# Who multiplies the modulation tiles, and where constants are made, in the opening of a decoder trunk

## The chip, the cores and the metric

One Trainium2 chip, one of its cores. The metric is the device time of one execution in microseconds (us); lower is better. TensorE is called PE here and in the profile (PEld is its weight load), VectorE DVE, ScalarE ACT, GpSimd POOL, SyncE SP.

## The reference, cut to what matters

One decoder layer over 2048 positions of 1024 channels, float32. Six modulation vectors come from the conditioning vector `c`; the first two, shift and scale, act on the input of the first projection:

```python
c_act = silu(c)                                  # 1024
mod = c_act @ ada_w + ada_b                      # ada_w: 1024 x 6144
sh1, sc1, g1, sh2, sc2, g2 = split(mod, 6)
h = rmsnorm(x, norm_mix_w) * (1.0 + sc1) + sh1   # 2048 x 1024
proj = h @ w_in                                  # split into eleven parts
# A: gated linear recurrence, B: sparse attention by an index score and top-k, C: convolution
x = x + g1 * (concat[o_a, o_b, o_c] @ w_out)
h = rmsnorm(x, norm_mlp_w) * (1.0 + sc2) + sh2
x = x + g2 * (relu(h @ mlp_w1)**2 @ mlp_w2)
out = rmsnorm(x, final_norm_w)
```

## The kernel before, in words

The 2048 positions go in four blocks of 512. Every large product is made of three rounded products: each operand is split into a high part, rounded for PE's fast float32 format by ACT, and a low part, what the rounding left. The low part of a weight tile (`wlo`, L318) is made by POOL; that of a slice of activations (`al`, L288) by DVE for slices 1, 4 and 6 and by POOL for the others.

**The opening** (block 0, before the projection runs). `in_norm` loads four tiles of x, and ACT, POOL and DVE normalise them. The scale `a1` and the shift `sh1` are columns of 128 channels by 8. `ada_half` makes half of one of them: eight tiles of `ada_w`, 128 rows by 512 columns, are multiplied by the matching column of `cact`, summed over the tiles and then over the rows. Before the change DVE multiplies and adds tile 0 and tiles 3 to 7 (`acc`, L238, L240). Tiles 1 and 2 (`AK`) are multiplied by ACT (L233) and added by POOL (L236). Then `part_sum` (L226) sums over the rows on PE: the tile is the stationary operand and a column of ones the moving one, four matmuls for 512 columns, each shown as two in the records. It runs twice in each half, once for POOL's tile and once for `acc`. DVE adds the bias (L244).

The order is: near half of the scale (`a1`, channels 0 to 511), near half of the shift (`sh`), then slices 0 to 3 of the input (`to_act_steps`: four transposes on PE, L281; scale and shift on ACT, `tf`, L286; rounding on ACT, `ah`, L287; low part). With them PE runs the first half of the channels of the first two projection units (`KO` = 2, L424). Then the far halves of scale and shift, slices 4 to 7, and the second half of these two units. `tf` has two buffers.

**The projection** of a block is a list of units, `in_units`: unit 0 the index key, 1 and 2 the index queries, 3 the forget gate of the recurrence's first head, 4 its query, 5 its values (wide), 6 its output gate, and so on. A unit fetches 512 KB of weights, ACT rounds them (L317), POOL makes their low parts, PE multiplies, ACT and DVE evacuate. `next_w` splits the weights of a unit about one unit ahead of its use. Rounded weights of block 0 are also written to DRAM (`wk_d`) for the later blocks. Behind unit 6 the recurrence of the first head starts in the background (`hgrn_gen`); it uses the masks `lmask`. The first top-k search (`topk_gen`) uses `zq` and `gq_`.

**Constants.** `late_consts`, called at unit 1, makes the constants of the search (`search_consts`: iota and two powers on POOL, some fifteen small DVE instructions), loads the convolution's taps, forms the bounds of the forget gate, and makes five masks: for each level DVE fills `mwork`, POOL selects twice (L514, L516), DVE casts into `lmask` (L518).

**Order.** The program is a list of instructions with tiles; a scheduler orders each engine's queue by a modelled timeline, taking the earliest instruction of the program that is ready, and tiles of one tag share a fixed number of buffers. So an instruction can stand well before its place in the program, and each queue then runs strictly in that order. DMAs are issued from SP, apart from a few small ones on ACT's queue.

Of the kernel before, what the change touches and what calls it, by code (L numbers as in the profile page):

```python
# [16 lines left out]
OP = mybir.AluOpType  # L17
# [26 lines left out]
KO, NPF = 2, 2  # L44
AK = [1, 2]
PTB, PM, LB, LB2 = 1, 1, 4, 4
# [32 lines left out]
def trunk(ctx, tc, x, c, ada_w, ada_b, norm_mix_w, norm_mlp_w, w_in, hg_lb_logits,  # L79
# [136 lines left out]
    def ada_half(sec, c0, dst, key, slots):  # L216
# [4 lines left out]

        side = []

        def part_sum(t, vec, first, last):
# [4 lines left out]
        for k in range(NK):  # L229
            t = slots[k]()  # L230
            dma(t, ada2[k * P:(k + 1) * P, sec * D + c0:sec * D + c0 + TB])
            if k in AK:
                A.mul(t, t, cact[:, k:k + 1])  # L233
                side.append(t)
                if len(side) > 1:
                    G.tensor_tensor(side[0], side[0], t, OP.add)  # L236
            elif k == 0:
                V.tensor_scalar(acc, t, cact[:, 0:1], None, op0=OP.mult)  # L238
            else:
                V.scalar_tensor_tensor(acc, t, cact[:, k:k + 1], acc, op0=OP.mult, op1=OP.add)  # L240
        if side:
            part_sum(side[0], ones[:, 0:1], True, False)
        part_sum(acc, ones[:, 0:1], not side, True)
        V.tensor_tensor(dst[:, t0:t0 + n], pt[:, :n], col("adab", sec * 8 + t0, n), OP.add)  # L244
# [29 lines left out]

    def to_act_steps(xh, acol, bcol, ah, al, mid=None):
        for k in range(NK):
# [10 lines left out]
            A.copy(hi, tf)  # L287
            (V if k in (1, 4, 6) else G).tensor_tensor(lo, tf, hi.bitcast(F32), OP.subtract)  # L288
            guard.__exit__(None, None, None)
# [176 lines left out]
    def search_consts():  # L466


        w = hp.tile([P, 5, 14], F32, tag="cu", bufs=2, name="sconst")
        ii = hp.tile([P, 14], mybir.dt.int32, tag="fb", bufs=FBB, name="sint")  # L470
        na, p_, q_, a_, b_ = [w[:, i] for i in range(5)]
# [21 lines left out]
    def late_consts():  # L493
        search_consts()
        cvrow = hp.tile([TAPS, 256], F32, tag="hc0", bufs=1, name="cvrow")
# [12 lines left out]

        mwork = hp.tile([P, 256], F32, tag="r", bufs=1, name="mwork")
        for l in range(5):  # L510
# [590 lines left out]
    def first_units(xts):  # L1101
        act = [], []
        steps = to_act_steps(xts, a1, sh1, *act)
        ws = []
# [14 lines left out]
    def in_block(b, xts, nxt):  # L1119
        act = first_units(xts) if b == 0 else to_act(xts, a1, sh1, lambda: pump("fast", rates["fast"]))  # L1120
        for u, (pieces, ev, m) in enumerate(in_units):
# [6 lines left out]
            if u == 1 and b == 0:  # L1128
                late_consts()
            if b == 0 and u < len(early):  # L1130
                ps = early[u]
# [537 lines left out]
```

## Time and profile before

| | us |
|---|---|
| median of 3 runs | 2896.21 |
| lowest, highest | 2892.06, 2897.85 |
| profiled execution, its time | 2887.88 |
| its span in the profile | 2886.1 |
| PE busy | 2757.0 (96%) |
| PEld busy | 2297.4 (80%) |
| DVE busy | 1671.6 (58%) |
| ACT busy | 1240.7 (43%) |
| POOL busy | 1086.6 (38%) |

The profiled execution is 8.3 us below the median of the runs. Busy time is an average over the whole span; the opening, where the change lies, is the first 70 us of it. Of the 40 slices of 72 us into which the page cuts the span, PE is busy five tenths in the first and nine or more in nearly all others.

### The profile page before, as it was taken

Reading aid. Unit: us, or ns where it says so; the run is one execution under the profiler, and the core shown is the slowest. Engines: PE = TensorE matmul, PEld = TensorE weight load, DVE = VectorE, ACT = ScalarE, POOL = GpSimd, SP = SyncE. Lnnn points to the kernel's source line nnn. Section 1 sums busy time; section 2 is a strip of 40 time slices with the busy share of each in tenths; the row PEclk is TensorE's granted clock in tenths of the full one; section 3 lists DMA queues with packets and bytes.
Section 4 is the critical chain, followed back from the end, with each engine's and each line's share of the span. In section 5 each row is a group of like instructions: output and inputs, shape, how many; then the busy total and the mean of one; then the engine's idle time right before and its main releaser. Section 6 shows DMA issues by size and latency. Waiting matters only on the chain.

```text
span 2886.1 us, 42799 instructions
## 1 busy us (share of the span) xinstructions
PE 2757.0 (96%) x14116; PEld 2297.4 (80%) x14116; DVE 1671.6 (58%) x3514; ACT 1240.7 (43%) x2630; POOL 1086.6 (38%) x1051
## 2 busy tenths in 40 slices
PE   5999998999999989999999999999999999999997
PEld 4888887888788777888777888888788887777876
DVE  6695697777465437657757637477662221254455
ACT  4436444533311354555556444354643333343333
POOL 7434111212100445666665222234422223345444
PEclk9999999999999989999999999999999999999999
DMA  8987676777555667889888776677867666686676
GB/s 292 293 270 248 216 233 195 221 222 248 190 187 179 224 223 252 282 287 288 291 271 290 237 223 213 208 248 257 285 219 234 204 225 204 219 283 210 229 238 207
DMA packets 428075, 688.62 MB, mean 239 GB/s; under 512 B 43384, under 2 KB 171453, under 8 KB 427837
## 3 DMA queue, kind: packets, MB, share of 16 engines
q1 hardware_dynamic: 427680, 685.67, 73.0%
q8 instruction: 113, 1.85, 0.3%
q14 instruction: 126, 1.02, 0.1%
q10 hardware_dynamic: 156, 0.07, 0.0%
HBM read 532.74 MB, written 152.84 MB: 238 GB/s over the span
## 4 chain that ended last, share of the span: by engine, by line
PE 45%; DMA 4%; DVE 4%; POOL 2%; issue 1%; ACT 1%; SPq 0%; POOLq 0%; DVEq 0%; ACTq 0%
PE mm L1306 11%; PE mm L424 10%; PE ax L424 7%; PE ax L1306 6%; PE mm L1466 3%; PE at L967 2%; PE po L1001 2%; PE at L989 1%; PE ix L809 1%; DMA wk<-wk_d 1%; DMA tr<-in_mlp_w_dram 1%; PE at L1306 1%; DVE s L816 1%; POOL wk L376 1%; DVE cum L919 1%
## 5 line engine op out<-in xcount | busy, mean ns | idle before, releaser
L424 PE MATMUL mm<-ah,wk 128*128 128x512 f32 x1920 | 509.4, 396 | 4.9 <-ACT tf L286 1.9
L424 PEld LDWEIGHTS mm<-ah,wk 128*128 128x128 f32 x1920 | 353.6, 188 | 77.7 <-ACT tf L286 2.1
L318 POOL TENSOR_TENSOR wlo<-wraw,whi 128x512 fp32r<-128x512 f32 x210 | 286.7, 1385 | 243.4 <-ACT whi L317 99.7
L999 POOL TENSOR_TENSOR pT<-L,pT 128x512 fp32r<-128x512 f32 (+3 forms) x160 | 192.9, 1207 | 371.8 <-ACT pT L998 203.1
L816 DVE SCALAR_TENSOR_TENSOR s<-r,iw_s,s 128x512 f32<-128x512 f32 (+3 forms) x266 | 237.4, 892 | 100.9 <-ACT r L811 92.8
L424 PE MATMUL mm<-al,wk 128*128 128x512 f32 x960 | 262.3, 395 | 0.0
L969 DVE CUSTOM_DVE_ANT_0 L<-at,bias 128x512 f32<-128x512 f32 (+3 forms) x152 | 93.7, 620 | 202.5 <-PE at L967 159.3
L424 PEld LDWEIGHTS mm<-al,wk 128*128 128x128 f32 x960 | 177.9, 188 | 35.4
L1306 PE MATMUL mm<-wk,hh 128*128 128x512 f32 x640 | 196.0, 395 | 2.1 <-ACT tf L286 1.1
L811 ACT ACTIVATE r<-ix 128x512 f32<-128x512 f32 (+3 forms) x256 | 133.3, 555 | 148.8 <-PE ix L809 99.9
L317 ACT CAST whi<-wraw 128x512 fp32r<-128x512 f32 x210 | 121.8, 621 | 159.7 <-DMA wraw<-in_mlp_w_dram 40.1
L273 POOL TENSOR_TENSOR hl<-hr,hh 128x512 fp32r<-128x512 f32 x96 | 128.5, 1340 | 159.9 <-ACT hh L265 158.1
L424 PE MATMUL ax<-ah,wk 128*128 128x512 f32 x720 | 185.4, 391 | 1.8 <-ACT hc L1440 1.4
L589 DVE SCALAR_TENSOR_TENSOR cx<-hc,cvc,cx 128x512 f32<-128x512 f32 x232 | 174.2, 751 | 2.0
L919 DVE TENSOR_SCALAR_CACHE_REDUCE cum<-s,ssm 128x384 bf16<-128x384 f32 (+13 forms) x112 | 165.4, 1477 | 8.2 <-POOL s L820 6.1
L997 ACT COPY L<-at 128x512 f32<-128x512 f32 (+3 forms) x160 | 82.9, 522 | 175.6 <-PE at L989 174.2
L424 PEld LDWEIGHTS ax<-ah,wk 128*128 128x128 f32 x720 | 134.1, 188 | 30.2 <-ACT hc L1440 1.8
L1466 PE MATMUL mm<-wk,hc 128*128 128x512 f32 x588 | 145.0, 392 | 6.9 <-DVE acc L1474 6.1
L983 ACT ACTIVATE L<-L,nmx 128x512 f32<-128x512 f32 (+3 forms) x160 | 103.8, 650 | 98.7 <-DVE nmx L978 98.4
L1306 PEld LDWEIGHTS mm<-wk,hh 128*128 128x128 f32 x640 | 118.0, 188 | 26.8 <-ACT tf L286 1.7
L1466 PEld LDWEIGHTS mm<-wk,hc 128*128 128x128 f32 x588 | 109.4, 188 | 34.1 <-DVE acc L1474 10.0
L1306 PE MATMUL ax<-wk,hh 128*128 128x512 f32 x384 | 122.6, 397 | 1.5 <-DMA wk<-wk_d 1.1
(364 smaller groups left out, 6077.8 us busy)
## 6 DMA issues: line engine op xcount, KB each, us to landing
wk<-wk_d SPq DMA_DIRECT2D x776, 256.0 KB
wk<-wk_d SPq DMA_DIRECT2D x196, 512.0 KB
wk_d<-whi SPq DMA_DIRECT2D x210, 256.0 KB
wk_d<-wlo SPq DMA_DIRECT2D x210, 256.0 KB
wraw<-in_mlp_w_dram SPq DMA_DIRECT2D x68, 512.0 KB
kc<-sk_d SPq DMA_DIRECT2D x112, 256.0 KB
vc<-v_d SPq DMA_DIRECT2D x112, 256.0 KB
adw<-in_ada_w_dram SPq DMA_DIRECT2D x128, 128.0 KB
```

What stands on the lines that cost most here:

```text
L273: e.tensor_tensor(lo[:, i:j], src[:, i:j], hi[:, i:j].bitcast(F32), OP.subtract)
L317: A.copy(hi, src)
L318: G.tensor_tensor(lo, src, hi.bitcast(F32), OP.subtract)
L424: T.matmul(ps, ww[k], aa[k], start=(n == 0 and k0 == 0), stop=(n == len(order) - 1 and k1 == NK))
L589: V.scalar_tensor_tensor(acc if w < TAPS - 1 else total, hc[:, w:w + TB], cvc[:, m, w:w + 1], acc, op0=OP.mult, op1=OP.add)
L811: A.activation(r[:, :w], ps[:, :w], AF.Relu, scale=32.0 ** -0.5)
L816: V.scalar_tensor_tensor(s[:, c0:c0 + w], r[:, :w], iw, s[:, c0:c0 + w], op0=OP.mult, op1=OP.add)
L919: V.tensor_scalar(dump, s, t, -AIM - i * STEP, op0=OP.is_ge, op1=OP.add, accum_out=d)
L983: A.activation(lt[:, :w], lt[:, :w], AF.Exp, bias=nmx, accum_out=sm[:, cb:cb + 1])
L999: G.tensor_tensor(pT[:, :nt, 1], lv, pT[:, :nt, 0].bitcast(F32), OP.subtract)
L1306: T.matmul(ps, aa[f][:, tok * P:(tok + 1) * P], ww[i], start=(first and n == 0), stop=(last and n == 5))
L1466: T.matmul(bank[t], aa[:, k, t * P:(t + 1) * P], ww[k], start=(i in (0, 2, 4) and n == 0), stop=(n == 5), skip_group_check=True)
```

## The change

PE multiplies tiles 1, 3, 5 and 7 of each half itself: `part_sum` runs on the tile as it was loaded, with the column of `cact` in place of the ones. ACT's multiplications and POOL's sums go; DVE keeps tiles 0, 2, 4 and 6. In block 0 DVE makes the low parts of all eight slices. `search_consts` and the masks (now `level_masks`) leave `late_consts` and are called at unit 4 of block 0; their work tiles take buffers of the tag `stg` (4 buffers, shared with the evacuations of keys and queries) in place of `cu`, `fb` and `r`.

```diff
-AK = [1, 2]
+AK = [1, 3, 5, 7]
...
             if k in AK:
-                A.mul(t, t, cact[:, k:k + 1])
-                side.append(t)
-                if len(side) > 1:
-                    G.tensor_tensor(side[0], side[0], t, OP.add)
+                part_sum(t, cact[:, k:k + 1], k == AK[0], False)
             elif k == 0:
                 V.tensor_scalar(acc, t, cact[:, 0:1], None, op0=OP.mult)
             else:
                 V.scalar_tensor_tensor(acc, t, cact[:, k:k + 1], acc, op0=OP.mult, op1=OP.add)
-        if side:
-            part_sum(side[0], ones[:, 0:1], True, False)
-        part_sum(acc, ones[:, 0:1], not side, True)
+        part_sum(acc, ones[:, 0:1], False, True)
...
-    def to_act_steps(xh, acol, bcol, ah, al, mid=None):
+    def to_act_steps(xh, acol, bcol, ah, al, mid=None, on_v=(1, 4, 6)):
...
-            (V if k in (1, 4, 6) else G).tensor_tensor(lo, tf, hi.bitcast(F32), OP.subtract)
+            (V if k in on_v else G).tensor_tensor(lo, tf, hi.bitcast(F32), OP.subtract)
...
-        w = hp.tile([P, 5, 14], F32, tag="cu", bufs=2, name="sconst")
-        ii = hp.tile([P, 14], mybir.dt.int32, tag="fb", bufs=FBB, name="sint")
+        w = hp.tile([P, 5, 14], F32, tag="stg", bufs=STG, name="sconst")
+        ii = hp.tile([P, 14], mybir.dt.int32, tag="stg", bufs=STG, name="sint")
...
     def late_consts():
-        search_consts()
...
-        mwork = hp.tile([P, 256], F32, tag="r", bufs=1, name="mwork")
+    def level_masks():
+        mwork = hp.tile([P, 256], F32, tag="stg", bufs=STG, name="mwork")
...
-        steps = to_act_steps(xts, a1, sh1, *act)
+        steps = to_act_steps(xts, a1, sh1, *act, None, range(NK))
...
             if u == 1 and b == 0:
                 late_consts()
+            if u == 4 and b == 0:
+                search_consts()
+                level_masks()
```

More of the change, by code (lines that the diff above doesn't have):

```diff
@@ L220, in ada_half @@
         t0 = c0 // P
-        side = []
         def part_sum(t, vec, first, last):
```

## The prediction

> **What bounds the kernel now.** I read the page first, then busy time by ten-microsecond stages, then the opening instruction by instruction, then the groups and waits of the stages behind it.
>
> ```profile
> span 2886.1 us, 42799 instructions
> 0.00:10.00 10.00, 0.24 (x1) 0.17 (x1) 1.97 (x15) 2.20 (x3) 6.86 (x13) 1.00 0.79 273
> 10.00:20.00 10.00, 3.15 (x13) 2.57 (x13) 7.35 (x15) 7.65 (x14) 9.04 (x11) 1.00 0.93 321
> 20.00:30.00 10.00, 6.08 (x28) 5.48 (x27) 8.54 (x17) 2.34 (x5) 6.03 (x7) 1.00 0.98 269
> 30.00:40.00 10.00, 5.53 (x21) 4.24 (x20) 8.87 (x8) 4.32 (x7) 8.73 (x7) 1.00 1.06 390
> 40.00:50.00 10.00, 9.79 (x50) 8.53 (x51) 9.05 (x17) 4.33 (x8) 6.43 (x4) 1.00 0.95 299
> 50.00:60.00 10.00, 5.78 (x29) 3.90 (x28) 7.44 (x15) 5.15 (x8) 7.68 (x5) 1.00 0.81 281
> 60.00:70.00 10.00, 9.82 (x36) 7.92 (x37) 4.44 (x7) 8.01 (x16) 6.70 (x10) 0.83 0.67 206
> 70.00:80.00 10.00, 10.00 (x48) 8.15 (x47) 5.00 (x7) 5.33 (x9) 5.89 (x7) 1.00 0.95 315
> 80.00:90.00 10.00, 10.00 (x81) 9.77 (x80) 3.00 (x7) 3.31 (x7) 3.91 (x4) 1.00 1.01 339
> ```
>
> Columns of a stage: length, busy us of PE, PEld, DVE, ACT and POOL with instruction counts, granted clock, DMA share, GB/s. From 70 us on TensorE is never idle, so what the opening saves is kept as long as weights, low parts and evacuations follow. Up to 60 us it is idle 29 of 60 us, while VectorE is at 7 to 9 tenths and the DMA engines near full. (The clock column reads 1.00 even there, yet a column sum takes 1.86 at 28 us and 0.95 at 48, next fence: the array runs at half its later speed.)
>
> The opening is a chain of three milestones: the near shift column `sh` (first halves of the sections), the far one, and the second half of the two early projection units.
>
> ```profile
> 11.49 1.32 ACT L233 ACTIVATE adw<-adw,cact 128x512 f32<-128x512 f32 x2
> 28.62 1.86 PE L226 MATMUL ax<-ones,adacc 128*128 128x1 f32 x8 [2.89 <-DVE adacc L240]
> 30.52 0.16 DVE L244 TENSOR_TENSOR sh<-ax,cols 128x4 f32<-128x4 f32 x1 [1.40 <-PE ax L226]
> 31.17 4.22 POOL L318 TENSOR_TENSOR wlo<-wraw,whi 128x512 fp32r<-128x512 f32 x3
> 32.50 5.11 DVE L240 SCALAR_TENSOR_TENSOR adacc<-adw,cact,adacc 128x512 f32<-128x512 f32 x3
> 37.53 1.75 DVE L288 TENSOR_TENSOR al<-tf,ah 128x512 fp32r<-128x512 f32 x1
> 39.38 0.78 ACT L286 ACTIVATE tf<-mm,sh,a 128x512 f32<-128x512 f32 x1 [4.91 <-DVE al L288]
> 48.31 0.95 PE L226 MATMUL ax<-ones,adw 128*128 128x1 f32 x8
> 50.19 0.16 DVE L244 TENSOR_TENSOR sh<-ax,cols 128x4 f32<-128x4 f32 x1 [0.91 <-PE ax L226]
> ```
>
> A row is start, length, engine, line, tile, count, and in brackets the idle time with what ended it. Near `sh` is done at 30.7, after a VectorE chain, a column sum on PE and a gap of 1.40. Then everything runs into VectorE and POOL: three multiply-adds take 5.11, 1.70 each, while POOL is busy; the low part on VectorE starts only at 37.53, and ACT waits 4.91 for it before it can scale slice two. Far `sh` comes at 50.19.
>
> ```profile
> 51.35 2.60 POOL L480 TENSOR_TENSOR sconst<-sconst 128x14 f32<-128x14 f32 x1
> 52.44 0.69 DVE L288 TENSOR_TENSOR al<-tf,ah 128x512 fp32r<-128x512 f32 x1 [0.78 <-ACT ah L287]
> 56.42 1.26 POOL L288 TENSOR_TENSOR al<-tf,ah 128x512 fp32r<-128x512 f32 x1
> 58.70 0.78 ACT L286 ACTIVATE tf<-mm,sh,a 128x512 f32<-128x512 f32 x1 [4.04 <-DVE gq__210 L488]
> 60.17 0.50 PE L424 MATMUL mm<-ah,whi 128*128 128x512 f32 x1 [3.75 <-ACT ah L287]
> 62.00:63.00 1.00, 1.00 (x4) 0.80 (x3) 0.57 (x1) 0.81 (x2) 0.39 (x1) 0.50 0.81 190
> ```
>
> Here the search constants are in the way. POOL spends 2.60 on each of two powers, then weight low parts, and reaches the low part of a slice at 56.42; VectorE's queue holds the constants' arithmetic, ACT waits 4.04 for it, PE waits 3.75, and the array, having been idle, comes back at a clock of 0.50.
>
> **The change part by part.** Durations come from the profiled execution: 2887.9 us beside a span of 2886.1. The median of the runs is 2896.2, so 8.3 is added at the end.
>
> ```profile
> L236 POOL TENSOR_TENSOR adw<-adw,adw 128x512 f32<-128x512 f32 x4 | 6.3, 1576 | 0.1
> L281 PE MATMUL mm<-ident,xt 128*128 128x128 f32 x32 | 7.8, 379 | 8.5 <-DVE xt L435 5.5 <-ACT tf L286 3.0
> L286 ACT ACTIVATE tf<-mm,sh,a 128x512 f32<-128x512 f32 x8 | 6.0, 774 | 12.4 <-DVE al L288 5.2 <-DVE gq__210 L488 4.0 <-DVE sh L244 3.2
> L287 ACT CAST ah<-tf 128x512 fp32r<-128x512 f32 x8 | 4.7, 618 | 0.2
> L514 POOL TENSOR_SCALAR_AFFINE_SELECT mwork<-mwork 128x256 f32<-128x256 f32 x5 | 6.4, 1278 | 4.8 <-DVE a L247 2.6 <-DVE mwork L513 2.1
> L516 POOL TENSOR_SCALAR_AFFINE_SELECT mwork<-mwork 128x256 f32<-128x256 f32 x5 | 5.8, 1165 | 0.2
> 67.63 1.98 PE L424 MATMUL mm<-ah,wlo 128*128 128x512 f32 x8
> 69.44 1.98 PE L424 MATMUL mm<-ah,whi 128*128 128x512 f32 x8
> ```
>
> Groups of the first 62 us: busy time, mean ns, idle before.
>
> *Multiplication of tiles.* Gone: 8 ACT multiplies (two took 1.32 at 11.49, so 5.3), 4 POOL adds (6.3), and 8 VectorE multiply-adds (six become four in each of four halves; up to 1.70 each). New: each half makes five column sums on PE where it made two, so 12 more in all. A sum is eight matmul records: 0.95 warm (48.31), 1.86 cold (28.62). No DMA is added, removed or moved past another, so the order of tiles on SP stays.
>
> *Near half.* Three ends. Arrival: x and the 16 near tiles are 6.3 MB; the first stages move 2.73 and 3.21 MB, so the last near tile lands at 21 to 23. With a warm array the last sums take 2 more: 25. With a cold one the queue of ten sums (18.6) and eight transposes of 0.38 (3.0) starts with the first odd tile, whose copy ACT took up at 11.49: 33. I take 26.5, nearer the warm end, and say below why: 4.0 earlier than 30.5.
>
> *Low parts on VectorE.* Five of eight move from POOL. At 52.44 VectorE needs 0.69, at 37.53 under a busy POOL 1.75. POOL still splits the weights of two units here, but has neither masks nor adds. The wait of 4.91 goes; late next is ACT, with (0.774+0.618) = 1.39 for each slice.
>
> *First half of the early units and the far half.* From 26.5+2.3 (scale, round, first matmul: 52.45 follows 50.19 in the same way) PE has 24 matmuls of 0.226 (8 of them from 67.63 to 69.44), ten sums of 0.97, and two slices' transposes at the warm rate (1.3): 5.4+9.7+1.3 = 16.4, hence far `sh` at 45.2 and not 50.2. This is a price PE didn't pay before, six sums or 5.8 of it. Ends: the far tiles' arrival (12.5 MB have moved by 40 us, the 8.4 MB of tiles, x and two units' weights are 11.5) plus two sums, 41; and, with near `sh` at 33 and half speed until 40, 53 (the 2.3 to the first matmul and the 4.7 behind it do 3.5 of the 16.4, and 12.9 are left). So 5.0 earlier in all, the first 4.0 included.
>
> *Second half.* The 3.75 wait goes with the constants. So does the slow clock behind it: a mean of 0.83 over 60 to 70 us is 1.7 lost. Late next is ACT: 1.39 for a slice against six matmuls (1.36); I leave 1.0 for that. Gain 4.5.
>
> Sum of the opening: 5.0+4.5 = 9.5 us by the time the early units end (about 67).
>
> *Constants and masks behind unit four.* They used to lie in the opening; now POOL has 6.4+5.8 of selects and 2×2.6 of powers, 17.4 in all, at about 70 to 95 us, where it makes the low parts of weights. In the new tag they wait until stores of the index queries have left its four buffers, and they stand in program order before that unit's weight splits.
>
> ```profile
> 78.36 2.80 POOL L318 TENSOR_TENSOR wlo<-wraw,whi 128x512 fp32r<-128x512 f32 x2 [4.11 <-ACT whi L317]
> 82.06 0.55 PEld L1282 LDWEIGHTS mm<-wlo,ah 128*128 128x128 f32 x4
> ```
>
> POOL finishes these two tiles at 81.16 and PE loads one at 82.06: a lead of 0.9. A power in front takes 2.6 out of that, the two selects of the first level 4.2. POOL is idle for 4.1 before 78.36, and 10 less the busy time of the stages 70 to 90 makes 10.2 in all. Queued behind on POOL are weight low parts only, and PE waits for them; on VectorE the mask's casts wait for POOL, with evacuations behind them that have a spare PSUM buffer. Ends: nothing, and 17.4-0.9 = 16.5. I take 1.5, since most of the powers fit the idle 4.1.
>
> *Transfers.* The opening's gain asks the same bytes in less time.
>
> ```profile
> ACT whi L317 <- PE mm L424: 18.8, 17, 3.1
> ACT whi L317 <- DMA wraw<-in_w_in_dram: 3.3, 2, 3.0
> ```
>
> Behind the opening the DMA share is 0.95 to 1.01. What can move up is the idle share of 40 to 80 us: 0.5+1.9+3.3+0.5 = 6.2. Of 9.5 that leaves 3.3 which PE could catch up with the stream. But the rounding of weights waited on PE 17 times (18.8) and on a transfer twice (3.3) between 62 and 182 us, so PE and not the stream set the pace. Ends 0 and 3.3; I take 0.8 on top of POOL's 1.5, since both delay the same matmuls.
>
> Net: 9.5-1.5-0.8 = 7.2. Profile 2887.9-7.2 = 2880.7; with 8.3, **2889.0**.
>
> **A warm or a cold array.** The near sums hang on this.
>
> ```profile
> 1033.62:1037.03 3.41, 3.41 (x19) 3.41 (x18) 1.23 (x4) 1.56 (x3) 1.27 (x1) 0.50 0.15 14
> 1037.03:1040.45 3.42, 3.42 (x18) 2.87 (x18) 1.62 (x4) 1.43 (x3) 1.53 (x1) 1.00 0.90 363
> 1036.04 1.48 PE L696 MATMUL ax<-q,k 128*128 128x64 f32 x8
> ```
>
> A stage of 3.41 filled without a gap by transposes and short 64-column matmuls ended with the clock going from 0.50 to 1.00. The near sums of the changed kernel fill PE just as densely (a cold one takes 1.86; an odd tile comes every 1.6 to 1.9, two of 262 KB at 321 or 269 GB/s), so I take them to warm it by about 20 us. The Trainium skill, "TensorE: Matmul & The Clock Gate", Part 1, says that about 3.4 us of sustained work releases the clock, but its Part 4 says that transposes don't count as such work. The stage above speaks against Part 4. No row shows one-column sums alone in such a stage; if they count as little as that page says of transposes, the cold rival below is what happens.
>
> The Trainium skill, "SBUF — State Buffer", section "Who interferes with whom", says that a VectorE instruction with two SBUF inputs and a POOL instruction that reads SBUF exclude each other for their whole length. The 1.75 against 0.69 agrees. By the rule alone each low part on VectorE would cost 1.75 wherever POOL splits weights; two on the path make 2.1 less gain, 2891.1.
>
> **The rivals.**
>
> *PE stays cold and becomes the opening's bound.* Near `sh` at 33, far at 53 (2.8 later), the second half still gains 4.5: net 1.7 before unit four's 1.5; the stream then costs nothing. Time about 2896. For it: PE stayed slow in every sum before 40 us. Against: the gaps between those, and the stage just shown.
>
> *The slower side: POOL at unit four.* If the selects and powers stand one behind another in front of the weight low parts, PE waits up to 16.5 where I count 1.5. It decides against the change from 8.7+5.8 = 14.5 on the path (the gain without that term, plus 0.2%); at 16.5, 2896.2-8.7+16.5 = 2904. For it: the lead of 0.9, and the fixed order. Against: the levels alternate with VectorE, which leaves POOL to the weights between them.
>
> *The constants don't move.* The scheduler had drawn them from unit one into the opening; with buffers of their new tag counted free it can do so again. Then the second half keeps its wait: 2896.2-5.0+0.8 = 2892. Against: the tag's earlier tiles belong to units before them.
>
> *More than expected.* Far `sh` by arrival (41, another 4.2) and nothing lost behind: 2896.2-13.7 = 2882.5.
>
> **How the numbers follow.** The forecast 0.44, with its own range 2886 to 2892 (nothing lost to the stream and little at unit four, or the whole 3.3 of the stream). Cold array 0.27 around 2896. POOL 0.13, from 2898 up to 2904. Constants unmoved 0.05, 2892. More 0.11, near 2882. Besides, the queues' order is worked out anew for the whole kernel, and a stall like the 3.75+1.7 can appear or go elsewhere: 5.5 either way, inside the range. Range 2882 to 2900, which leaves out about 2 in 10: part of the best case, part of POOL's. About 0.2%, 5.8 us, is what measurement can tell from no change; so faster means under 2890.4: most of the forecast (0.38) and all of the better case, with a little of the unmoved: 0.50. Slower, over 2902: most of POOL's and a little else, 0.13. Same: 0.37.
>
> **What would show it.** Near `sh` at 25 to 28 and far at 44 to 47; column sums of 0.95 before 25 us (1.8 would be the cold rival). ACT's wait for a low part on VectorE under 1.5, not 4.91. No PE gap over 2 us between 50 and 62, and no clock of 0.50 there. TensorE continuously busy from about 44, not 60. At unit four: PE waiting on weight low parts for more than 3 us in total, or powers and selects directly in front of them on POOL, would show its rival; weight rounding waiting often on transfers before 115 us would show the stream. I am wrong if the early units end less than 3 us earlier, or if they do and the gain is gone by 120 us.

## The result, and the profile after

The changed kernel is slower: 2913.65 us (median of 5; lowest 2905.35, highest 2918.50) beside 2894.95 for the kernel before on the same chip, a ratio of 1.0057 [1.0037, 1.0077]. A second time it was 2908.65 beside 2896.81, 1.0040 [1.0018, 1.0062]. 2889.0 had been predicted, with a range to 2900. The rows below are of the execution of 2905.35 us. Lines from about 245 to 1120 of the changed file stand 7 or 8 lower than before (L424 is L417, L288 is L281, L643 is L636), later ones 4 (L1282 is L1278).

The page's first line, then stages (columns as in the prediction), of the changed kernel:

```profile
span 2903.6 us, 42969 instructions
20.00:30.00 10.00, 10.00 (x49) 10.00 (x49) 3.25 (x6) 2.27 (x4) 3.83 (x3) 1.00 1.06 299
30.00:40.00 10.00, 10.00 (x42) 9.32 (x42) 7.65 (x12) 4.94 (x8) 1.74 (x2) 1.00 1.05 392
50.00:60.00 10.00, 5.56 (x28) 4.35 (x28) 3.41 (x8) 3.45 (x6) 0.00 (x0) 0.57 0.68 197
60.00:70.00 10.00, 10.00 (x35) 8.00 (x34) 4.30 (x6) 7.74 (x15) 4.30 (x9) 0.74 0.62 246
80.00:90.00 10.00, 5.33 (x28) 4.34 (x26) 5.10 (x7) 6.34 (x10) 10.00 (x6) 0.95 0.98 331
90.00:100.00 10.00, 7.33 (x44) 7.34 (x45) 7.25 (x23) 0.90 (x3) 1.88 (x3) 0.71 0.62 181
```

PE is full from 20 to 50 us, as was wanted, and it brings nothing: from 50 to 70 us the mean clock is 0.57 and 0.74 (1.00 and 0.83 before), and a new hole stands at 80 to 100, where PE had been full.

The opening of the changed kernel, PE's rows and then VectorE's:

```profile
21.22 6.96 PE L224 MATMUL ax<-cact,adw 128*128 128x1 f32 x32
40.77 0.60 PE L417 MATMUL at<-ah,whi 128*128 128x512 f32 x1
41.20 0.41 PE L417 MATMUL at<-al,whi 128*128 128x512 f32 x1
46.12 3.71 PE L224 MATMUL ax<-cact,adw 128*128 128x1 f32 x32
55.29 1.20 PE L417 MATMUL at<-ah,whi 128*128 128x512 f32 x2
58.98 0.79 PE L417 MATMUL at<-al,whi 128*128 128x512 f32 x1 [2.49 <-DVE al L281]
33.00 0.15 DVE L237 TENSOR_TENSOR sh<-ax,cols 128x4 f32<-128x4 f32 x1
56.80 1.52 DVE L199 SCALAR_TENSOR_TENSOR adacc<-adw,cact,adacc 128x256 f32<-128x256 f32 x3 [4.08 <-DMA adw<-in_ada_w_dram]
58.24 1.28 DVE L281 TENSOR_TENSOR al<-tf,ah 128x512 fp32r<-128x512 f32 x2
```

The 32 records of 21.22 take 0.218 each: 1.74 for a tile's eight, the price of a cold array, although PE has had no gap since 11.49. The records' spacing shortens only behind 4.4 us of products of 512 columns: 0.60 at 40.77, 0.41 at 41.20. Warm, the 32 records of 46.12 take 0.93 for eight; then the clock falls again (0.60 for a product at 55.29). Near `sh` stands at 33.15 and far `sh` at 52.71. Then PE waits 2.49 for a low part that VectorE makes at 58.24: three background multiply-adds (L199), one waiting for a tile, stand ahead of it in VectorE's queue.

Unit four of the changed kernel, ScalarE, VectorE, POOL, PE:

```profile
80.49 1.14 ACT L310 CAST whi<-wraw 128x512 fp32r<-128x512 f32 x2 [5.12 <-DMA wraw<-in_w_in_dram]
82.95 0.60 ACT L624 ACTIVATE f<-mm 128x512 f32<-128x512 f32 x1
84.76 1.17 DVE L628 TENSOR_SCALAR f<-f 128x512 f32<-128x512 f32 x1 [5.47 <-ACT f L625]
87.38 2.04 DVE L705 TENSOR_TENSOR fb<-fb 128x128 f32<-128x128 f32 x3
89.48 2.53 DVE L705 TENSOR_TENSOR fb<-fb 128x16 f32<-128x16 f32 x3
91.93 0.68 DVE L636 SCALAR_TENSOR_TENSOR q<-mm,u 128x512 f32<-128x512 f32 x1
81.81 2.60 POOL L473 TENSOR_TENSOR sconst<-sconst 128x14 f32<-128x14 f32 x1
84.37 2.69 POOL L311 TENSOR_TENSOR wlo<-wraw,whi 128x512 fp32r<-128x512 f32 x2
87.02 2.31 POOL L509 TENSOR_SCALAR_AFFINE_SELECT mwork<-mwork 128x256 f32<-128x256 f32 x1
89.31 2.48 POOL L311 TENSOR_TENSOR wlo<-wraw,whi 128x512 fp32r<-128x512 f32 x2
92.67 1.23 PE L1278 MATMUL mm<-whi,ah 128*128 128x256 f32 x4 [7.33 <-DVE q L636]
```

PE stands for 7.33 us, waiting for the query `q`. Backwards: `q` (91.93) is behind six products of the forget gate's powers (L705) on VectorE, which take 4.6 together, over three times their price in another kernel (e2, below), beside POOL's weight low parts and one mask fill; POOL's two powers are over by 84.41. These products wait for the gate `f`; and `f` (82.95) stands in ScalarE's queue behind the rounding of a weight tile that waited 5.12, by this profile for its transfer. Behind the hole PE runs at half clock: the stage 90 to 100 has a mean of 0.71.

To compare kernels I count the products of weights with activations in the trace, in order of time, and take the difference of the n-th's start to that of before (good to about half a microsecond). The 64th ends the early units; the 100th, 150th and 200th lie about unit four (77.0, 85.1 and 91.1 us before). The changed kernel is 3.3 us late at the 64th and 100th, 14.0 at the 150th, 15.4 at the 200th. So the first condition under which the prediction called itself wrong came true: the early units end late, and there was no gain to lose behind them.

Such a difference is not all loss. From the 64th to the 200th product the changed kernel takes 12.1 longer: PE stands 7.3, the products themselves take 1.2 more, and 3.6 go to 20 more records of other products (the recurrence's and the index score's), which the kernel before runs behind its 200th. This last part is work moved, not work lost.

### The profile page after: what moved, and what is told of

It is laid out like the page before. It is cut to its first block, busy times and chain, and to the rows that moved or that the text cites. A ratio compares the mean times of both kernels' runs of the same rounds, so it can differ in the third digit from the quotient of the medians.

```text
span 2903.6 us, 42969 instructions
## 1 busy us (share of the span) xinstructions
PE 2778.8 (96%) x14212; PEld 2318.5 (80%) x14212; DVE 1675.8 (58%) x3511; ACT 1240.5 (43%) x2626; POOL 1070.7 (37%) x1042
## 4 chain that ended last, share of the span: by engine, by line
PE 42%; DVE 4%; DMA 4%; POOL 1%; issue 1%; ACT 0%; SPq 0%; POOLq 0%; DVEq 0%; ACTq 0%
PE mm L1302 10%; PE mm L417 9%; PE ax L417 7%; PE ax L1302 5%; PE mm L1462 4%; DMA wk<-wk_d 2%; PE po L994 1%; PE at L960 1%; PE at L982 1%; PE ix L802 1%; PE at L1302 1%; DVE cum L912 1%; DVE s L809 1%; DMA tr<-in_mlp_w_dram 1%; DMA wraw<-in_mlp_w_dram 1%
## 5 line engine op out<-in xcount | busy, mean ns | idle before, releaser
L417 PE MATMUL mm<-ah,wk 128*128 128x512 f32 x1920 | 509.4, 396 | 2.6 <-DVE slo L531 0.9
L417 PEld LDWEIGHTS mm<-ah,wk 128*128 128x128 f32 x1920 | 353.7, 188 | 74.6 <-issue 1.3
L417 PE MATMUL mm<-al,wk 128*128 128x512 f32 x960 | 261.5, 394 | 0.0
L417 PEld LDWEIGHTS mm<-al,wk 128*128 128x128 f32 x960 | 177.7, 188 | 35.7
L417 PE MATMUL ax<-ah,wk 128*128 128x512 f32 x720 | 185.4, 391 | 1.4 <-ACT hc L1436 1.4
L417 PEld LDWEIGHTS ax<-ah,wk 128*128 128x128 f32 x720 | 134.3, 188 | 29.4 <-ACT hw L1424 1.8
L1462 PEld LDWEIGHTS mm<-wk,hc 128*128 128x128 f32 x588 | 109.3, 188 | 34.0 <-DVE acc L1470 10.7
```

The lines of the kernel that those rows point to most:

```text
L417: T.matmul(ps, ww[k], aa[k], start=(n == 0 and k0 == 0), stop=(n == len(order) - 1 and k1 == NK))
L1462: T.matmul(bank[t], aa[:, k, t * P:(t + 1) * P], ww[k], start=(i in (0, 2, 4) and n == 0), stop=(n == 5), skip_group_check=True)
```

## The experiments

Part A is the multiplication of tiles on PE, B the low parts on VectorE, C the constants and masks behind unit four. Before each run two theories were set down: P (each part has its own loss) and Q (the queues are drawn anew); later ones are named where they come up.

| kernel | near `sh` | far `sh` | 64th | 200th | ratio to before |
|---|---|---|---|---|---|
| before (time 2893.6 to 2898.2) | 30.68 | 50.35 | 0 | 0 | 1 |
| before again (e11) | 30.43 | 50.15 | -0.4 | -0.4 | 0.9997 [0.9979, 1.0015] |
| A (e1) | 32.56 | 55.50 | +0.3 | +7.9 | 1.0048 [1.0031, 1.0064] |
| B (e2) | 30.35 | 49.58 | -4.8 | -4.8 | 0.9979 [0.9966, 0.9992] |
| B again (e14) | 30.65 | 51.18 | -3.5 | -3.4 | 1.0000 [0.9986, 1.0014] |
| C (e3) | 27.68 | 47.18 | -7.6 | -0.3 | 0.9995 [0.9982, 1.0009] |
| A+B (e4) | 33.35 | 54.03 | +3.6 | +6.5 | 0.9996 [0.9986, 1.0006] |
| A+C (e8) | 34.06 | 51.53 | +3.1 | +17.3 | 1.0043 [1.0029, 1.0057] |
| B+C (e5) | 26.95 | 45.74 | -8.3 | +1.2 | 1.0015 [1.0002, 1.0028] |
| A+B+C, the change | 33.15 | 52.71 | +3.3 | +15.4 | 1.0057 [1.0037, 1.0077] |
| the change again (e17) | 33.47 | 52.91 | +2.4 | +15.9 | 1.0040 [1.0018, 1.0062] |
| B, search constants late (e7) | 30.30 | 50.79 | -4.1 | -1.9 | 1.0009 [0.9998, 1.0020] |
| B, masks late (e16) | 27.14 | 45.93 | -7.9 | -4.1 | 0.9976 [0.9961, 0.9990] |
| the same again (e18) | 27.17 | 45.93 | -9.0 | -4.0 | 0.9968 [0.9952, 0.9984] |

**How well a profile repeats.** e11 (no edit) and e17 (no edit of the changed kernel):

> The kernel before once more, unchanged, for a second profile of it: its profiled execution of 2887.9 us lay 7 us under the median of its other runs, and this shows in which stretch two profiles of the same kernel part. Theory L (the opening and unit four repeat to within half a microsecond, and the executions part behind 300 us): the first 300 heavy products lie within 0.5 us of the first profile. Rival (the opening itself varies by some microseconds): they do not, and differences between kernels in the first 100 us must be read with that spread.

> The changed kernel once more, for a second profile of it. If its opening and unit four repeat as those of before did: the 64th heavy product 3 to 4 us late against before, the 150th 13 to 15, the near shift at 33.0 and the far one at 52.6 within 0.3 us, the time 2905 to 2919. If the stall at unit four is a matter of one execution, the 150th stands elsewhere by 3 us or more.

Two profiles of before agree within 0.5 us for the first 800 products (231 us) and part behind: 4.5 at the 1000th, 6.9 at the 2000th, 11.3 at the 8000th. The changed kernel's two agree within about 1.4 up to the 200th, and PE's wait for `q` is 7.3 and 7.2. So the opening and unit four belong to the kernel and are read to about a microsecond (B's 64th moved by 1.3), while the ends of two profiles can't be compared. Medians of a dozen runs can.

**One part at a time** (e1, e2, e3, e4; all edits here are cut to the lines that matter):

```diff
e1  -AK = [1, 2]                    +AK = [1, 3, 5, 7]      # and part_sum on the loaded tile
e2  -to_act_steps(..., *act)        +to_act_steps(..., *act, None, range(NK))
e3  +if u == 4 and b == 0: search_consts(); level_masks()   # out of late_consts, work tiles in tag stg
e4  e1 and e2
```

> The kernel before, with the multiplication of tiles 1, 3, 5 and 7 given to TensorE, and nothing else changed. Theory P (each part has its own loss): the 40 column sums of the two near halves and the first of the far ones run at half speed, so near sh comes at 31 to 33 and far sh at 51 to 54, as in the changed kernel (33.0 and 52.6); the early units end some 3 us late and there is no gap over 2 us at units four and five: before plus 2 to 5. Theory Q (the queues drawn anew are the loss, whatever the part): ACT's queue has the rounding of unit five's weights ahead of the forget gate here too, waits for the transfer, and TensorE stands 5 us or more at unit five: before plus 8 or more.

> The kernel before, with all low parts of block 0's slices on VectorE, and nothing else changed. Theory P: the opening is 1 to 4 us shorter (the wait of 4.91 for the low part goes, the constants' wait of 3.75 stays), no new gap behind it: before minus 3 to plus 1. Theory Q: ACT's queue has the rounding ahead of the forget gate here as well; TensorE stands 3 us or more around unit five: before plus 3 to 8.

> The kernel before, with the search constants and the masks made behind unit four as in the changed kernel, and nothing else changed. Theory P: the opening gains 3 to 6 us (no powers and masks in it), but POOL is full behind unit four, VectorE's instructions beside it stretch, and TensorE stands 5 to 9 us at units four to six and comes back at half speed: before plus 3 to 9. Theory Q: the rounding on ACT is drawn between the forget gate's instructions here, so that its evacuation is on time: the opening's gain is kept, before minus 3 to 6.

> The changed kernel with the search constants and the masks put back at unit one (sums on TensorE and low parts on VectorE remain). Theory P: the 11 us that TensorE loses around unit five go, the loss of 3 in the opening stays or grows by the constants' wait: before plus 2 to 7. Theory Q: ACT's rounding stands ahead of the forget gate as in the changed kernel, so most of the 11 us stay: before plus 10 to 16.

A alone cost 14.9 us (2913.01 beside 2898.15), B alone gained 4.2, C moved nothing, A+B neither. Neither theory held. P had the sign of A and of B, but not their size (it gave A a loss of 2 to 5 and B a gain of at most 3). Q had A's time, not its mechanism: PE's longest wait at units four and five is 2.1, where it foresaw 5 or more. On C and A+B both missed. A's loss is not that of the late opening either: its 64th product is 0.3 late, 7.6 come by the 200th, and 7.0 behind that, where no cause was found. C gained 7.6 in the opening and was 7.3 later again by the 200th product; PE stands for 2.9 of these, and 3.1 are other work moved ahead.

**Pairs** (e5: the change without A; e8: without B; e7: B with `search_consts` alone at unit four):

```diff
e7  +if u == 4 and b == 0: search_consts()                  # level_masks stays in late_consts
```

> The changed kernel without its first part: VectorE makes the low parts and the constants and masks stand behind unit four, but of the modulation tiles TensorE multiplies none and the old pair on ScalarE and GpSimd stays. Theory S (the loss is that of the sums on the cold array; the other two parts each took nothing or gained): the opening ends 7 us early, unit four gives a part back, and the time is 4 to 8 us below before, 2890 to 2894. Theory O (the loss is the place of the constants and masks once the work of ScalarE and VectorE is ahead of it: ScalarE's rounding waits for a transfer in front of the forget gate, and VectorE's powers run beside GpSimd's mask fills): the 150th heavy product comes 8 us or more later against before than the 100th, and the time is 2899 to 2908.

> The changed kernel with the old places of the low parts (GpSimd makes five of eight). Theory S: the two parts add up, 2913 less the 1 us of the constants alone: 2910 to 2914. Theory O: the unit-four loss of the changed kernel (11 us between the 100th and the 150th heavy product) stands here too and comes on top of the first part's late opening: 2913 to 2920, with 8 us or more between those two products.

> The kernel before with VectorE's low parts, and only the search constants behind unit four; the masks stay in the opening, TensorE multiplies none of the modulation tiles. Theory O: without the mask fills GpSimd is free at unit four, VectorE's powers take 0.55 to 0.7 us each again, so the opening's gain is kept: the 150th heavy product is no later against before than the 100th by more than 1.5 us, and the time is 3 to 9 us below before, 2889 to 2895. Rival (whatever is put behind unit four costs there as much as it freed): as the low parts alone or a little more, 2894 to 2898.

e5 reads as if the prediction had been made for it: near `sh` 26.95 (26.5 predicted), far 45.74 (45.2), the 64th product 8.3 earlier (9.5). It does so without A, with its sums on a cold array and VectorE multiplying as before. C's move alone gives 27.68 and 47.18. So what the prediction credited to the tiles on PE comes from taking the masks out of the opening (e7, which leaves them there, has near `sh` at 30.30); A, added to any of these, takes it away (near `sh` 33 to 34 in e8 and both timings of the change). The time of e5, 2899.47 beside 2893.64, is still theory O's: what it gained is gone by the 200th product, though in a slope and not in one stall (3.5 between the 100th and the 150th). e8, 2909.30, has the stall that O foresaw (12.6 between these two), at a time just under both S and O.

Between the 64th and the 200th product C costs 7.3 alone, 9.5 with B, 6.6 more than A alone, 9.2 more than A+B. Of the 9.5, PE stands for 4.0 and 3.8 are other work moved ahead. A alone costs 7.6 there, of which PE's waits make 4.6 (2.1 for a low part of the index queries, 1.4 for `q`, 0.7 and 0.4 for ScalarE). In e7 the search constants alone cost 2.2, without a stall between the 100th and the 150th product, as O said; its time of 2897.70 is the rival's.

**Are the sums slow because of the clock?** e6 adds wide products that nobody reads; e9 turns the sums round; e12 is e9's form with A+B.

```diff
e6  +for _ in range(36): T.matmul(pdum[:, :256], dum[:, :P], dum, start=True, stop=True)
     part_sum(t, cact[:, k:k + 1], k == AK[0], False)
    +for _ in range(2): T.matmul(pdum[:, :P], ident, t[:, :P], start=True, stop=True)
e9  -for i in range(n): T.matmul(pt[:, i:i + 1], t[:, i * P:(i + 1) * P], vec, ...)
    +T.matmul(pt[0:1, :TB], vec, t, start=first, stop=last)
    +V.tensor_copy(acc[0:1, :], pt[0:1, :TB])               # then four small products to columns
```

> The changed kernel with added products whose results nobody reads: 36 of 256 columns at the start, and two of 128 columns behind the sums of each tile that TensorE multiplies. Theory H (one-column sums, though TensorE is never idle among them, do not release its clock; wide products do): the clock is up by 20 us, the 8 records of a tile's sums take 0.93 to 1.0 us in place of 1.74 to 1.86, the near shift stands at 25 to 28.5 in place of 33.0 and the far one at 45 to 49 in place of 52.6. Rival (the sums are slow for another reason: the tiles' arrival, or the weight loads beside the transfers): the records stay at 1.74 us or more although the added products run at the full clock, and both shifts come later than in the changed kernel by the added products' 10 us or so. The end tells less, since unit four is left as it was: 2905 to 2914 by H, 2914 to 2925 by the rival.

> The changed kernel with the sums on TensorE laid the other way round: cact (or the column of ones) is the held operand and the tile streams past it, 512 columns in one product in place of four products of one column; the row of 512 is copied out by VectorE and turned into four columns by four small products at the end of each half. Theory H (the clock follows the columns that stream, not how long TensorE is busy; weight loads with one column behind them do not release it): such products take about 2 us cold, the clock is released within some 6 us of them, by 25 us, and then each takes about half; the near shift stands at 26 to 30 (33.0 in the changed kernel) and the far one at 46 to 50 (52.6); the 64th heavy product comes 3 to 7 us earlier than in the changed kernel. The stall at unit four is left as it is, so the time is 2904 to 2911. Rival (the held operand has one column, so nine tenths of the array are idle and the clock stays at one half): the products take about 2 us to the end, the near shift is no earlier than 35 and the time is 2913 to 2922.

> The kernel before with the first part in the wide form (tiles streaming past cact) and with VectorE's low parts; constants and masks stay in the opening. By Theory H the floor under the opening goes with the cold sums and no constants stand at unit four: the 64th heavy product comes 0 to 5 us earlier than before's, and the time is 2888 to 2895. By the rival of the cold row products the opening ends 3 us or more late, and the time is 2898 to 2905.

e6, two stages and rows of PE:

```profile
12.96:13.45 0.49, 0.49 (x7) 0.49 (x5) 0.13 (x1) 0.49 (x1) 0.49 (x1) 1.00 1.00 364
13.50:14.00 0.50, 0.50 (x5) 0.50 (x4) 0.24 (x1) 0.36 (x1) 0.34 (x2) 0.50 0.97 328
12.96 0.66 PE L229 MATMUL ax<-cact,adw 128*128 128x1 f32 x5
13.48 2.06 PE L229 MATMUL ax<-cact,adw 128*128 128x1 f32 x9
```

The 36 products released the clock. The first five sums, at a clock of 1.00, follow each other by about 0.11; from 13.48, at 0.50, the next nine do by 0.21. The same instruction, half the speed: it is the clock, which answers the rival. But theory H's numbers failed here (near `sh` 36.01, far 64.64): the mixture of sums and two products of 128 columns a tile stayed at 0.50 from 16 to 36 us with PE full, and the added work made it 2929.23, 1.0114 [1.0094, 1.0135], over both forecasts. What lowered the clock at 13.48 e6 doesn't say, since PE had stood 2.67 and 0.92 shortly before. The changed kernel's second profile (e17) does:

```profile
45.69 3.71 PE L224 MATMUL ax<-cact,adw 128*128 128x1 f32 x32
49.27 1.38 PE L224 MATMUL ax<-ones,adacc 128*128 128x1 f32 x8
49.20:49.70 0.50, 0.50 (x6) 0.50 (x7) 0.29 (x3) 0.00 (x0) 0.00 (x0) 1.00 1.07 391
49.90:50.40 0.50, 0.50 (x4) 0.50 (x5) 0.26 (x1) 0.00 (x0) 0.00 (x0) 0.50 0.45 160
```

Here PE runs nothing but one-column sums from 45.55 on, without a gap, and the clock falls from 1.00 to 0.50 before 49.9. In e9, PE:

```profile
12.62 3.57 PE L223 MATMUL ax<-adw,cact 128*1 128x512 f32 x4
18.76 1.02 PE L223 MATMUL ax<-adw,cact 128*1 128x512 f32 x2
30.27 1.86 PE L223 MATMUL ax<-adw,cact 128*1 128x512 f32 x2 [3.01 <-DVE sh L239]
```

A tile of 512 columns costs 1.8 cold (3.57 for two) and is warm by 18.76, 0.9 apart: streaming columns release the clock though the held operand has one column. The Trainium skill, "TensorE: Matmul & The Clock Gate", Part 1, gives about 3.4 us of sustained work for this, in a window that does not start with the work; here some 5 us passed from 12.62. Near `sh` is 30.19, better than the change by 3.0 and just over H's range, far `sh` 53.13 is not: between the halves PE waits 3.01 and the clock is lost once more (30.27: 1.86 for one tile). Still the 64th product is 1.2 ahead of before and 4.5 ahead of the change, and the time 2897.01, 1.0004 [0.9989, 1.0020], below H's: with A's sums wide the loss is gone within the error, although the stall at unit four is left. e12 gave 3.0 ahead at both counts and 2895.71, 1.0000 [0.9984, 1.0016]; A in the better form adds nothing to B. (C's price is still 9.6 in e9, from -1.2 to +8.4.)

**What makes the stall at unit four?** e10 ties ScalarE's two roundings behind the gate and the query; e15 is e10 and e9 together; e13 is e5 with two mask fills in place of ten.

```diff
e10 -A.copy(hi, src)
    +A.activation(hi, src, AF.Identity, bias=after_f[:, 0:1])   # a zero made from the gate's k, then from u
e13 +if l: V.tensor_copy(lmask[:, l, :], mwork); continue
```

> The changed kernel with one thing tied: ScalarE's rounding of the weight tiles for units six and seven takes a bias of zero that is made from the forget gate's and the query's results, so that it can no longer stand ahead of them in ScalarE's queue. Nothing else is moved. Theory O (the wait for q at unit four is in its larger part the rounding's wait for a transfer ahead of the forget gate): the wait of 7.3 us falls to 2 to 4, the 150th heavy product comes 6 to 8 us against before instead of 14, and the time is 4 to 6 us under the changed kernel's, 2905 to 2910. Rival (VectorE beside GpSimd sets it, the gate's place doesn't matter, or the weights of the next unit are late in its place): the 150th product stays at 12 to 15 us and the time at 2911 to 2917.

> The changed kernel with both mends: the sums laid the other way round, as in e9, and ScalarE's two roundings tied behind the forget gate and the query, as in e10. If the cold sums and the gate's place behind the transfer are all of the loss: the 64th heavy product at 0 to 2 us ahead of before's, the 200th no later than before's, the time 2889 to 2893. If GpSimd's work at unit four is a price of its own: the 200th at 5 to 9 us late as in e9, where the gate had no transfer to wait for, and the time 2894 to 2900.

> The kernel of e5 (low parts on VectorE, constants and masks behind unit four, no tiles on TensorE) with only the first level's mask filled by GpSimd, two fills in place of ten; VectorE copies it for the other four levels. It leaves out the masks of four levels. Theory W (the price at unit four is GpSimd's work, and what VectorE loses beside it): e5 lost 4.5 us between its 64th and its 150th heavy product, beside two powers and two fills, and 5.0 between the 150th and the 200th, beside the later fills; here the first stays within 1.5 us of that and the second falls to 0 to 2; the 200th product stands at 2 to 5 us earlier than before's, and the time is 2891 to 2897. Theory O (the price is the queues drawn anew, which are drawn the same here up to the later fills): both losses stay, the 200th product is 0 to 2 us late, and the time is 2896 to 2902.

e10: the wait of 7.3 is gone, the 150th product is 10.8 late in place of 14.0 (O gave 6 to 8) and the 200th 11.2 in place of 15.4; the time is 2901.70, 1.0016 [1.0000, 1.0032], below both forecasts. From the 100th (2.1 late) to the 200th it falls back by 9.1 where the change did by 12. PE stands 3.0 of these in place of 7.3, 2.8 of it for a transfer of the index queries; 5.2 in place of 3.6 are other work moved ahead. So tying ScalarE's order took 4.3 off PE's standing. The time fell by more (12.0 and 7.0 under the change's two timings). e15 went the wrong way: 2.9 ahead at the 64th, 15.9 late at the 200th, 2919.57, 1.0073 [1.0057, 1.0090]. PE stands 8.5 in between (4.4 for `q`, a wait of 3.9 for the index scores) and is at half clock from 83.3 to 100.4. Its wait for `q`, and rows of ScalarE, VectorE and POOL:

```profile
PE mm L1290 <- DVE q L648: 4.4, 1, 4.4
73.93 0.82 ACT L633 ACTIVATE f<-f,lbc,oml 128x512 f32<-128x512 f32 x1
77.33 0.17 DVE L474 CAST sconst<-sint 128x14 f32<-128x14 int32 x1 [4.56 <-DMA iq_d<-slo]
78.33 2.01 DVE L478 TENSOR_SCALAR sconst<-sconst 128x14 f32<-128x14 f32 x1
79.71 0.89 DVE L636 TENSOR_SCALAR f<-f 128x512 f32<-128x512 f32 x1
81.10 1.38 DVE L717 TENSOR_TENSOR fb<-fb 128x128 f32<-128x128 f32 x6
80.28 2.77 POOL L480 TENSOR_TENSOR sconst<-sconst 128x14 f32<-128x14 f32 x1
83.08 0.24 DVE L484 RECIPROCAL sconst<-sconst 128x14 f32<-128x14 f32 x1 [0.60 <-POOL sconst L480]
83.24 0.63 DVE L648 SCALAR_TENSOR_TENSOR q<-mm,u 128x512 f32<-128x512 f32 x1
```

ScalarE has the gate ready at 74.75, but VectorE takes it up only at 79.71. In front of it in VectorE's queue stands the first of the search constants (L474), which waits 4.56 for a store of the index queries to leave its buffer, and the constants behind that, one of which takes 2.01 beside a mask fill. A reciprocal (L484) that waits for POOL's power, until 83.05, adds only 0.60, and `q` starts right behind it. That is a third road from C to the same stall, and no tie on ScalarE touches it. e13 leaves out the masks of four levels (it copies the first level's in their place). The two powers and first two fills stay, and the price stays too (64th -9.9, 200th +3.2; 2905.12, 1.0028 [1.0013, 1.0044]): theory W's numbers, by which the later fills make the second part of it, fail (4.5 to the 150th as it said, then 8.6 in place of 0 to 2), and O's time is passed too. This doesn't settle W, because e13 has a wait of its own: VectorE's copies for the other levels stand ahead of the first reader of the mask.

```profile
PE ax L699 <- DVE at L680: 4.0, 1, 4.0
```

What VectorE loses beside POOL, in e5 (four fills and powers, then low parts of weights on POOL), against the kernel of e2, which has nothing of C there:

```profile
88.59 4.20 DVE L816 SCALAR_TENSOR_TENSOR s<-r,iw_s,s 128x384 f32<-128x384 f32 x3
89.52 2.86 POOL L318 TENSOR_TENSOR wlo<-wraw,whi 128x512 fp32r<-128x512 f32 x2
```
```profile
90.52 0.62 DVE L816 SCALAR_TENSOR_TENSOR s<-r,iw_s,s 128x384 f32<-128x384 f32 x1
76.69 1.39 DVE L712 TENSOR_TENSOR fb<-fb 128x128 f32<-128x128 f32 x6
```

1.40 for a multiply-add with two tiles in place of 0.62; the six powers' products take 1.39 together in e2, and 4.6 in the changed kernel (2.04+2.53). The Trainium skill, "SBUF — State Buffer", section "Who interferes with whom", states the lock between the two engines; these rows agree. The rows of e15 agree only in part: beside POOL's power, which reads SBUF too, the six products keep their price (1.38 at 81.10).

**A version below both** (e14 is e2 again; e16 and e18 are B with only the masks behind unit four):

```diff
e16 +if u == 4 and b == 0: level_masks()                    # search_consts stays in late_consts
```

> The kernel of e2 (only the second part, VectorE's low parts) once more. If its gain is that of the opening (4.8 us up to the 500th heavy product, kept to the end): 3 to 7 us below before. If the first interval was luck, within 2 us of before. In the profile the 64th heavy product stands 4.3 to 5.3 us ahead of before's first profile, as it did.

> Low parts on VectorE and the masks alone behind unit four; the search constants stay in the opening, and TensorE multiplies no tile. Of the kernels with low parts on VectorE, between the 64th and the 200th heavy product against before, the one with neither lost 0, the one with the search constants alone behind unit four 2.2 us, the one with both 9.5. Theory V (the price is the chain of constants, VectorE's queue standing at an operation that waits for GpSimd's power with work for TensorE behind it, made worse by fills ahead of the second power): without powers there the masks cost 0 to 3 us in that stretch. Theory M (the masks themselves cost: their first reader follows within 15 us, and it waits for fills that stand between the low parts of weight slices): 5 to 8 us in that stretch.

> The kernel of e16 once more. If its gain is real: the ratio to before under 0.9990 again, the time 4 to 9 us below before's, and in the profile the 64th heavy product 7.4 to 8.4 us and the 200th 3.6 to 4.6 us ahead of before's. If the first interval was luck: within 2 us of before.

B alone was not confirmed: 2895.14 beside 2895.70, and 3.5 ahead at the 64th. e16 was: 2889.35 beside 2896.81, then 2888.57 beside 2896.84, 8.3 us. Of the opening's 7.9 it keeps 4.1 at the 200th, of 9.0 in the second profile 4.0. Its price of 3.8 lies between theories V and M, and 5.0 in e18 at M's lower end, so the two are not decided. 2.2 (constants) and 3.8 or 5.0 (masks) make 6.0 to 7.2 where both together cost 9.5; but PE's standing adds up (1.6 in e7, 1.9 and 3.2 in e16 and e18, 4.0 in e5), and the rest is mostly the 3.8 of moved work. Rows of VectorE and POOL in e16, and PE's wait there and in e18:

```profile
72.85 4.61 DVE L713 TENSOR_TENSOR fb<-fb 128x128 f32<-128x128 f32 x6
71.09 2.88 POOL L318 TENSOR_TENSOR wlo<-wraw,whi 128x512 fp32r<-128x512 f32 x2
PE mm L1285 <- DVE q L644: 0.7, 1, 0.7
PE mm L1285 <- DVE q L644: 2.0, 1, 2.0
```

The gate's powers run beside POOL here as well (4.61, and 5.84 in e18), but no search constant stands in VectorE's queue and the gate is on time, and PE waits 0.7 and 2.0. So the stretched powers alone don't make the 7.3.

## Why the prediction was wrong

- **Warming the near sums** failed. From a stage of transposes and 64-column products the prediction said of the sums: "so I take them to warm it by about 20 us". PE was as full as in that stage and stayed at half speed to 41 us. The cold rival's 33 and 53 were met by 33.15 and 52.71, with 1.74 a tile where it said 1.8. The Trainium skill, "TensorE: Matmul & The Clock Gate", Part 4, says that transposes don't count as work for the clock; here one-column sums behave so, and the sentence of the prediction that named this as the open point was the one to weigh more.
- **Near half, 4.0 earlier**: in the change it is 2.5 later. That e5, without A, meets the number is luck, because the cause is another: VectorE's chain before 30.5 us was slow because of the masks, not because it had multiply-adds too many. C alone has near `sh` at 27.68, and the masks alone move it from 30.35 (B) to 27.14 (e16), with every multiply-add in place. The masks lengthen the chain in two ways whose shares were not measured: VectorE fills, converts and waits for them itself, and its instructions stretch beside POOL's fills. Rows of before, and the second instruction in e16:

```profile
17.51 1.32 POOL L514 TENSOR_SCALAR_AFFINE_SELECT mwork<-mwork 128x256 f32<-128x256 f32 x1
17.98 1.39 DVE L435 TENSOR_SCALAR xt<-xt,rs 128x1024 f32<-128x1024 f32 x1
18.18 0.75 DVE L435 TENSOR_SCALAR xt<-xt,rs 128x1024 f32<-128x1024 f32 x1
```

- **The wait of 4.91** for a low part in the near half was credited to B. In B alone it is 3.83; with C alone it is 2.11 (e3), with both 1.91 (e5). B's 4.8 come in the far half: the 25th product, the first of that half, stands 0.3 ahead, the 48th 4.4. ScalarE's row in e2:

```profile
37.98 1.44 ACT L286 ACTIVATE tf<-mm,sh,a 128x512 f32<-128x512 f32 x2 [3.83 <-DVE al L288]
```

- **Second half, gain 4.5**: in the change it is a loss. The constants' wait went, but a low part behind background multiply-adds took 2.49 of it, and the slow clock that was to go grew (0.57 and 0.74 in the two stages). Even the cold rival, which kept this gain, was therefore 5.0 too good at the 64th product (1.7 ahead foreseen, 3.3 late measured).
- **Unit four, 1.5** measured 10.7 by the 150th product and 12.1 by the 200th, inside its ends (0 to 16.5), nearer the upper one; PE stands for 7.3 of it. The rival put the wait at weight low parts on POOL; it came at `q`. Of the prediction, the step that failed here is "with evacuations behind them that have a spare PSUM buffer": `q` is the operand of the next product, so no spare buffer helps. Three roads lead there: ScalarE's rounding in front of the gate (PE stands 4.3 less with it tied behind, e10), VectorE's powers stretched beside POOL (4.6 for 1.39; alone they leave a wait of 0.7 and 2.0, e16 and e18), and, seen only in e15, the constants' wait for their buffer in front of the gate in VectorE's queue. How much each carries in the changed kernel was not separated.
- **Transfers, 0.8**: no stream limit shows. The 5.12 in the first of those roads is put down to one transfer, issued at 73.80 where before issues it at 70.69; in e17 the same wait, 5.24, is put down to a product that frees the rounded tile's buffer, so which of the two holds it stays open.
- The sum: 9.5 gained became 3.3 lost (12.8), unit four took 10.6 more than counted by the 200th product, and the 0.8 for transfers is inside that: 2889.0+12.8+10.6-0.8 = 2911.6, beside 2913.65 and 2908.65. Behind the 200th product the kernels gain or lose up to some 7 us in the end (A+B: 6.5 late there, no loss in the time; A: 7.9 late there, 14.9 lost). Moved work can explain gains only. The cause of these shifts stays open.

## What to carry to other kernels

A PE that is busy is not a PE that is warm: before moving small reductions to it, look whether rows of exactly that shape have ever run at full clock, and if they must move, let the data stream past a held vector. When an engine gets less work and nothing becomes faster, look for what ran beside it: here the masks, not the sums on VectorE, were the price of the opening. Work moved out of a crowded stage is not free where it lands: ask for each in-order queue what stands in front of the next product's operand, and for what that waits in its turn, a buffer included. Move pieces apart and time each: the masks alone behind unit four made the only kernel here that was below before twice (by 7.5 and 8.3 us).

## What the runs showed of the hardware

One-column sums, with some transposes between them and PE's record full from 11.49 to 36 us, kept a spacing of 0.218 where the warm array has 0.116. Nothing but such sums from 45.55 on lowered a clock that was up (1.00 at 49.7, 0.50 at 49.9, e17). Rows of 512 columns with one held column released it in some 5 us (e9). The clock column reads 1.00 ahead of the first change that it records, so up to 41 us of the changed kernel the records' spacing is the only clock. VectorE's products with two inputs in SBUF take over three times as long beside POOL's low parts and fills (4.6 for 1.39), but not beside its power (1.38).
